# A memory gain carried as a 769th column, a rope table loaded last, and row blocks turned between two halves of a product

## The chip, the core and the metric

The kernel runs on one core of one Trainium2 chip. The core has a matrix engine (TensorE, PE in the rows; its weight loads are PEld), a vector engine (VectorE, DVE), a scalar engine (ScalarE, ACT), GpSimd (POOL), a queue engine that issues most transfers (SyncE, SP), and 16 DMA engines. The engines run their own instruction streams in order and wait for one another through semaphores. The metric is device time of one execution in microseconds (us). Before the change: 756.78 us, the median of three runs (756.1, 756.78, 756.96).

## What is computed

One decoder layer for 512 tokens of width 1024, in fp32. Cut to what the change touches:

```
h = rms_norm(x, g_mix)
q, k, v, qi, ki, wi, conv_in, qc, gate_pre = split(h @ w_in)
qi = partial_rope(qi);  ki = partial_rope(ki)          # index heads, first 8 of 32 columns turned
mem_kv = rms_norm(mem, g_mem) @ w_mem_kv                # 256 memory tokens
... sparse attention, short convolution, memory attention, gates, w_o, gated MLP, final norm
```

`rms_norm` multiplies a row by 1/sqrt(mean of squares) and by a gain per column. In the memory product the gain can sit on the contraction index, and the factor of the row can wait until after the product.

## The kernel before, in words

Every product is done with split operands: a number is kept as a rounded high part and a low rest (`split`, L155: a copy on ScalarE, then a subtraction on VectorE), and `mm3` (L145) adds three products per contraction chunk, high by high, high by low, low by high. Contraction runs over 8 chunks of 128.

The first 50 us are a start-up stage, in which SyncE's queue brings, in this order: the memory chunks `m_kv` (8 chunks, each 256 columns of the turned memory and 512 of its weights, 768 columns of 128 rows), row block 0 of x, the gain `g_mix` for all partitions (`gx`), row block 1, the weights `w_n` of the small projection (v, the index queries and keys and the index weights: 424 columns), row block 2, memory rows 0, row block 3, memory rows 1, and `par`. ScalarE's own queue issues two small transfers first: the memory gain `gm` (128 x 8, L231) and the rope table `ropeN` (128 x 32, L232).

The compute of that stage:

- For each memory chunk, ScalarE and VectorE scale it by `gm` (L280, L281) into `mT`, the weights are split, and TensorE adds to `ps_o` and `ps_mm` (L287).
- A row block of x is normalized by `norm_rows` (L165): ScalarE squares it and sums (L160), GpSimd makes the factor in two instructions (L161, L162), VectorE multiplies (L170) into `xn`. Then `turn_rows` (L173) lets TensorE transpose it, four 128 x 128 pieces at a time into a PSUM bank (`ps_at`), and splits each four into `hhi` and `hlo`.
- The loop at L321 runs over the four row blocks b. It multiplies block b by `w_n`, 8 chunks of three matmuls into `pn` (`ps_mm`, 128 x 424), and normalizes and turns block b + 2 at high priority (L329). Then it takes v and `wiN` from `pn`, copies the 288 index columns to `rn` (L335), turns the first eight of every 32 by the rope table in six small VectorE instructions (L338 to L343), and transposes `rn` on TensorE (L346, L349). For b below 2, `memory_out` (L296) squares and sums a block of memory rows and scales the memory product's results (`kr`, `vm`).

The tile `st`, which holds a row sum and its factor, has two buffers, and so has `xn`. A scheduler puts the instructions of each engine into one fixed order from its own estimate of times; `tc.high_priority` moves work up in it, and `tc.keep_in_program_order` pins an instruction to the written order. At run time each engine follows its list, whatever comes late.

After this stage come the rest of the projection (w_in), the attentions, the gates, w_o, and the MLP.

Of the kernel before, what the change touches and what calls it, by code (L numbers as in the profile page):

```python
# [10 lines left out]
F32 = mybir.dt.float32  # L11
F32R = mybir.dt.float32r
AF = mybir.ActivationFunctionType
ALU = mybir.AluOpType
# [3 lines left out]
P = 128  # L18
# [13 lines left out]
M = 256  # L32
# [41 lines left out]
class Late:  # L74
# [5 lines left out]
    def add(self, fn, extra=0):  # L80
        self.queue.append((self.now + self.lag + extra, fn))
# [9 lines left out]


@with_exitstack
def layer(ctx, tc, x, mem, g_mix, g_mem, g_ffn, g_final, w_in, w_n, m_kv, w_cm, w_att, w_o, w_up, w_down,
          params, rope, rope_n, out):
    nc = tc.nc

# [8 lines left out]
    def bank(tag="mm"):  # L106
        return ps.tile([P, 512], F32, tag=tag, name="ps_" + tag, bufs=banks[tag])
# [34 lines left out]
    def wrows(w, r, sp=wp):  # L142
        return wsplit(w[r * P:(r + 1) * P, :].rearrange("p (k c) -> p k c", c=P), sp)

    def mm3(o, sh, sl, mh, ml, first, last):  # L145
        nc.tensor.matmul(o, sh, mh, start=first, stop=False)  # L146
        nc.tensor.matmul(o, sh, ml, start=False, stop=False)  # L147
        nc.tensor.matmul(o, sl, mh, start=False, stop=last)  # L148

# [5 lines left out]
    def split(hi, lo, src):  # L155
        nc.scalar.activation(hi, src, AF.Copy)  # L156
        nc.vector.tensor_sub(lo, src, hi.bitcast(F32))  # L157
# [7 lines left out]
    def norm_rows(src, g, tmp):  # L165

        xn = tmp.tile([P, D], F32, tag="xn", name="xn", bufs=2)
        st = tmp.tile([P, 2], F32, tag="st", name="st", bufs=2)
        r = inv_rms(src, st, xn)
        nc.vector.scalar_tensor_tensor(xn, src, r, g, op0=ALU.mult, op1=ALU.mult)  # L170
        return xn

    def turn_rows(xn, dst, b, tag="at"):  # L173

        for h in range(2):
            pt = bank(tag)
            for k in range(4):
                nc.tensor.transpose(pt[:, k * P:(k + 1) * P], xn[:, (4 * h + k) * P:(4 * h + k + 1) * P], ident)
            pv = pt.rearrange("p (k s) -> p k s", s=P)
            split(dst[0][:, 4 * h:4 * h + 4, b * P:(b + 1) * P], dst[1][:, 4 * h:4 * h + 4, b * P:(b + 1) * P], pv)  # L180

    def norm_T(src, g, dst, b, tmp):
        turn_rows(norm_rows(src, g, tmp), dst, b)
# [41 lines left out]

    es = ExitStack()
    ea = es.enter_context(pool("ea", side="right"))
    gm = ea.tile([P, KD], F32, name="gm")
    gx = ea.tile([P, D], F32, name="gx")
    ropeN = ea.tile([P, 2, NB, 4], F32, name="ropeN")  # L230
    nc.scalar.dma_start(gm, g_mem)  # L231
    nc.scalar.dma_start(ropeN, rope_n)  # L232

    warm = const.tile([P, 1], F32, name="warm")
    tc.keep_in_program_order(nc.scalar.activation(warm, mhalf, AF.Copy))
# [2 lines left out]
    def first(dma):  # L238
        tc.keep_in_program_order(dma)

    def first_rows(src, b, p, tag):
        t = p.tile([P, D], F32, tag=tag, name="rows")
        first(nc.sync.dma_start(t, src[b * P:(b + 1) * P, :]))
        return t
# [5 lines left out]
    for c in range(KD // 2):  # L250

        n = 1 if c == 0 else 2
        raw = op.tile([P, 2, M + 2 * CW], F32, tag=kv_tags[c], name="mkv")
        for i in range(0, 2, n):
            first(nc.sync.dma_start(raw[:, i:i + n], m_kv[2 * c + i:2 * c + i + n].rearrange("k p c -> p k c")))
        hi = wp.tile([P, 2, 2 * CW], F32R, tag="whi", name="whi", bufs=3)
        lo = wp.tile([P, 2, 2 * CW], F32R, tag="wlo", name="wlo", bufs=3)
        mkv.append((raw, hi, lo, n))
        if c == 2:
            xin = [first_rows(x, 0, ea, "in0")]  # L260
            first(nc.sync.dma_start(gx, bcast(g_mix, D)))
# [8 lines left out]
    memn = [first_rows(mem, 0, op, "omeh")]  # L270
    xin.append(first_rows(x, 3, ea, "in3"))
    memn.append(first_rows(mem, 1, op, "omel"))


    pkv = [bank("o"), bank()]
    for c, (raw, hi, lo, n) in enumerate(mkv):
        for i in range(0, 2, n):
            for k in range(2 * c + i, 2 * c + i + n):
                src = raw[:, k % 2, :M]
                nc.scalar.activation(mh[:, k], src, AF.Copy, scale=gm[:, k:k + 1])  # L280
                nc.vector.scalar_tensor_tensor(ml[:, k], src, gm[:, k:k + 1], mh[:, k].bitcast(F32), op0=ALU.mult,  # L281
                                               op1=ALU.subtract)
            split(hi[:, i:i + n], lo[:, i:i + n], raw[:, i:i + n, M:])
            for k in range(2 * c + i, 2 * c + i + n):
                for b in range(MB):
                    bs = slice(b * P, (b + 1) * P)
                    mm3(pkv[b], mh[:, k, bs], ml[:, k, bs], hi[:, k % 2], lo[:, k % 2], k == 0, k == KD - 1)  # L287
        if c == 2:
            norm_T(xin[0], gx, h, 0, ea)
# [31 lines left out]
    for b in range(NB):  # L321
        bs = slice(b * P, (b + 1) * P)
        pn = bank()
        for i in range(4):
            for j in range(2):
                k = 2 * i + j
                mm3(pn[:, :NW], h[0][:, k, bs], h[1][:, k, bs], wn[i][1][:, j], wn[i][2][:, j], k == 0, k == KD - 1)
        if b + 2 < NB:
            with tc.high_priority(offset=800):  # L329
                norm_T(xin[b + 2], gx, h, b + 2, ea)  # L330
        split(V[:, b, :, 0:HD], V[:, b, :, HD:], pn[:, :KV].rearrange("p (g d) -> p g d", g=NG))
        nc.vector.tensor_scalar_mul(wiN[:, b, :], pn[:, NW - NIH:NW], (NIH * IDXD) ** -0.5)
        rn = ea.tile([P, NIH + 1, IDXD], F32, tag="rn", name="rn", bufs=2)
        rt = ea.tile([P, 2, NIH + 1, 4], F32, tag="rt", name="rt", bufs=2)
        nc.scalar.activation(rn, pn[:, KV:NW - NIH].rearrange("p (n d) -> p n d", d=IDXD), AF.Copy)  # L335
        cos, sin = (ropeN[:, i, b:b + 1, :].to_broadcast([P, NIH + 1, 4]) for i in range(2))
        a1, a2 = rn[:, :, 0:4], rn[:, :, 4:8]
        nc.vector.tensor_mul(rt[:, 0], a2, sin)  # L338
        nc.vector.tensor_mul(rt[:, 1], a1, sin)
        nc.vector.tensor_mul(a1, a1, cos)  # L340
        nc.vector.tensor_mul(a2, a2, cos)
        nc.vector.tensor_sub(a1, a1, rt[:, 0])
        nc.vector.tensor_add(a2, a2, rt[:, 1])  # L343
        rows_ = rn.rearrange("p n d -> p (n d)")
        pt = bank("at")
        nc.tensor.transpose(pt[:IDXD, 2 * P:3 * P], rows_[:, 2 * P:], ident)  # L346
        if b:
            for t in range(2):
                nc.tensor.transpose(pt[:, t * P:(t + 1) * P], rows_[:, t * P:(t + 1) * P], ident)  # L349
        nc.scalar.activation(rK[:, bs], pt[:IDXD, 2 * P:3 * P], AF.Copy)  # L350
        if b:
            nc.scalar.activation(rQ[:, :, (b - 1) * P:b * P], pt[:, :2 * P].rearrange("p (t s) -> p t s", t=2), AF.Copy)
        if b < MB:
            memory_out(b, kr[:, b])
        if b:
            ahead(C_CG if b == 1 else C_U if b == 2 else C_BG)
# [512 lines left out]
```

## Time and profile before

| | |
|---|---|
| median of three runs | 756.78 us |
| the profiled execution | 757.61 us |
| its span on the core | 755.8 us |
| PE busy | 740.9 us (98%), 3458 matmuls and transposes |
| DVE, ACT, POOL busy | 464.5, 340.2, 21.1 us |
| HBM read | 75.77 MB |

The profile is one execution of the program. The span is what the core's trace covers; the execution's time is 1.8 us more. A busy TensorE is not a TensorE at its peak: matmuls overlap, and their ends are modelled, so the distance from one start to the next says what one costs. An idle engine costs time only if the chain that ends last runs through the wait.

### The profile page before, as it was taken

Reading aid. Unit: us, or ns where it says so; the run is one execution under the profiler, and the core shown is the slowest. Engines: PE = TensorE matmul, PEld = TensorE weight load, DVE = VectorE, ACT = ScalarE, POOL = GpSimd, SP = SyncE. Lnnn points to the kernel's source line nnn. Section 1 sums busy time; section 2 is a strip of 40 time slices with the busy share of each in tenths; the row PEclk is TensorE's granted clock in tenths of the full one; section 3 lists DMA queues with packets and bytes.
Section 4 is the critical chain, followed back from the end, with each engine's and each line's share of the span. In section 5 each row is a group of like instructions: output and inputs, shape, how many; then the busy total and the mean of one; then the engine's idle time right before and its main releaser. Section 6 shows DMA issues by size and latency. Waiting matters only on the chain.

```text
span 755.8 us, 9168 instructions
## 1 busy us (share of the span) xinstructions
PE 740.9 (98%) x3458; PEld 618.9 (82%) x3458; DVE 464.5 (61%) x795; ACT 340.2 (45%) x568; POOL 21.1 (3%) x49
## 2 busy tenths in 40 slices
PE   6999999999999999999999999999999999999996
PEld 4888888888888888888899888888888888888884
DVE  4845999999777763386466565656565654121225
ACT  5848565676455553244235434343434443121214
POOL 0200002000000000000010000000000000000001
PEclk9999999999999999999999999999999999999998
DMA  9625234522122224344403232232323232323202
GB/s 340 221 84 172 85 111 123 170 72 76 57 91 74 74 65 161 117 139 138 142 29 99 97 97 100 91 104 88 107 86 110 83 112 76 119 84 109 86 29 112
DMA packets 25709, 81.81 MB, mean 108 GB/s; under 512 B 3424, under 2 KB 4576, under 8 KB 25664
## 3 DMA queue, kind: packets, MB, share of 16 engines
q1 hardware_dynamic: 25232, 80.94, 32.7%
q8 instruction: 27, 0.44, 0.3%
q10 hardware_dynamic: 432, 0.28, 0.1%
q14 instruction: 18, 0.15, 0.1%
HBM read 75.77 MB, written 2.10 MB: 103 GB/s over the span
## 4 chain that ended last, share of the span: by engine, by line
PE 94%; ACT 2%; DMA 1%; DVE 1%; POOL 1%; issue 1%; POOLq 0%; SPq 0%
PE ps_mm L146 19%; PE ps_mm L148 19%; PE ps_mm L147 19%; PE ps_at L146 9%; PE ps_at L148 9%; PE ps_at L147 9%; PE ps_at L625 1%; PE ps_o L656 1%; DMA mkv<-m_kv 1%; PE ps_o L147 1%; PE ps_o L148 1%; PE ps_o L146 1%; PE ps_at L642 1%; PE ps_at L420 1%; PE ps_at L556 1%
## 5 line engine op out<-in xcount | busy, mean ns | idle before, releaser
L157 DVE TENSOR_TENSOR wlo<-raw,whi 128x1024 fp32r<-128x1024 f32 (+2 forms) x122 | 144.7, 1188 | 197.1 <-ACT whi L156 197.1
L156 ACT ACTIVATE whi<-raw 128x1024 fp32r<-128x1024 f32 (+2 forms) x122 | 125.8, 1032 | 177.1 <-PE ps_o L148 82.1
L146 PE MATMUL ps_mm<-hhi,whi 128*128 128x512 f32 x312 | 122.8, 394 | 0.0
L147 PE MATMUL ps_mm<-hlo,whi 128*128 128x512 f32 x312 | 122.2, 392 | 0.0
L148 PE MATMUL ps_mm<-hhi,wlo 128*128 128x512 f32 x312 | 122.2, 392 | 0.0
L147 PE MATMUL ps_at<-h2l,whi 128*128 128x512 f32 (+1 forms) x216 | 78.9, 366 | 0.0
L148 PE MATMUL ps_at<-h2h,wlo 128*128 128x512 f32 (+1 forms) x216 | 78.8, 365 | 0.0
L146 PE MATMUL ps_at<-h2h,whi 128*128 128x512 f32 (+1 forms) x216 | 78.7, 366 | 0.0
L148 PEld LDWEIGHTS ps_mm<-hhi,wlo 128*128 128x128 f32 x312 | 58.6, 188 | 11.7
L147 PEld LDWEIGHTS ps_mm<-hlo,whi 128*128 128x128 f32 x312 | 58.6, 188 | 11.6
L146 PEld LDWEIGHTS ps_mm<-hhi,whi 128*128 128x128 f32 x312 | 58.6, 188 | 11.5
L146 PE MATMUL ps_mm<-h2h,whi 128*128 128x512 f32 x160 | 62.2, 389 | 0.0
L147 PE MATMUL ps_mm<-h2l,whi 128*128 128x512 f32 x160 | 62.2, 389 | 0.0
L148 PE MATMUL ps_mm<-h2h,wlo 128*128 128x512 f32 x160 | 62.2, 389 | 0.0
L147 PEld LDWEIGHTS ps_at<-h2l,whi 128*128 128x128 f32 x216 | 40.7, 189 | 6.6
L148 PEld LDWEIGHTS ps_at<-h2h,wlo 128*128 128x128 f32 x216 | 40.7, 189 | 6.5
L146 PEld LDWEIGHTS ps_at<-h2h,whi 128*128 128x128 f32 x216 | 40.6, 189 | 6.5
L147 PEld LDWEIGHTS ps_mm<-h2l,whi 128*128 128x128 f32 x160 | 30.0, 188 | 6.3
L148 PEld LDWEIGHTS ps_mm<-h2h,wlo 128*128 128x128 f32 x160 | 30.0, 188 | 6.2
L146 PEld LDWEIGHTS ps_mm<-h2h,whi 128*128 128x128 f32 x160 | 30.0, 188 | 6.2
L789 ACT ACTIVATE t<-t 128x512 f32<-128x512 f32 x22 | 13.9, 633 | 44.9 <-DVE t L471 44.8
L156 ACT ACTIVATE acth<-t 128x512 fp32r<-128x512 f32 x14 | 8.8, 632 | 40.4 <-DVE t L790 40.4
(266 smaller groups left out, 1316.8 us busy)
## 6 DMA issues: line engine op xcount, KB each, us to landing
raw<-w_up SPq DMA_DIRECT2D x44, 512.0 KB, 3.4
raw<-w_in SPq DMA_DIRECT2D x39, 512.0 KB, 3.4
raw<-w_down SPq DMA_DIRECT2D x22, 512.0 KB, 3.4
raw<-w_o SPq DMA_DIRECT2D x8, 512.0 KB, 3.5
raw<-w_cm SPq DMA_DIRECT2D x8, 320.0 KB, 3.0
mkv<-m_kv SPq DMA_DIRECT2D x3, 768.0 KB, 8.8
rows<-x SPq DMA_DIRECT2D x4, 512.0 KB, 10.1
x<-x SPq DMA_DIRECT2D x4, 512.0 KB, 6.4
```

The source lines that it names most:

```text
L146: nc.tensor.matmul(o, sh, mh, start=first, stop=False)
L147: nc.tensor.matmul(o, sh, ml, start=False, stop=False)
L148: nc.tensor.matmul(o, sl, mh, start=False, stop=last)
L156: nc.scalar.activation(hi, src, AF.Copy)
L157: nc.vector.tensor_sub(lo, src, hi.bitcast(F32))
L420: nc.tensor.matmul(pb[:, :W], Q4[:, hd, (b - 1) * P:b * P], K4[:, :W], start=True, stop=True)
L556: nc.tensor.matmul(pb[:, j * M:(j + 1) * M], QC[:, 2 * t + j, b * P:(b + 1) * P], KM[i][:, 2 * t + j, :], start=(i == 0), stop=(i == 1))
L625: nc.tensor.matmul(pb[:, :N], QS[:, hd, b * P:(b + 1) * P], KS[i][:, g, :N], start=(i == 0), stop=(i == 1))
L642: nc.tensor.transpose(pt[:, kb * P:(kb + 1) * P], lt[:, kb * P:(kb + 1) * P], ident)
L656: nc.tensor.matmul(po[:, q0:], V[:, kb, g, :], PT[i][:, c], start=(kb == 0 and i == 0), stop=(kb == NB - 1 and i == 1))
L789: nc.scalar.activation(tt[0], tt[0], AF.Silu)
```

## The change

The memory gain becomes column 768 of each memory chunk, so a chunk has 769 columns, and the transfer of `gm` is gone. `ropeN` is loaded by SyncE's queue after memory rows 1. In the loop over row blocks, block b + 1 (for b = 1 and 2) is normalized at the top of step b at high priority, and its transposes are written between chunks 0 to 3 and chunks 4 to 7 of the product of block b; the first transpose of each four and the first matmul of chunk 4 are pinned to the written order.

```diff
-    gm = ea.tile([P, KD], F32, name="gm")
...
-    nc.scalar.dma_start(gm, g_mem)
-    nc.scalar.dma_start(ropeN, rope_n)
...
-        raw = op.tile([P, 2, M + 2 * CW], F32, tag=kv_tags[c], name="mkv")
+        raw = op.tile([P, 2, M + 2 * CW + 1], F32, tag=kv_tags[c], name="mkv")
...
     memn.append(first_rows(mem, 1, op, "omel"))
+    first(nc.sync.dma_start(ropeN, rope_n))
...
-                src = raw[:, k % 2, :M]
-                nc.scalar.activation(mh[:, k], src, AF.Copy, scale=gm[:, k:k + 1])
...
+                src, gm = raw[:, k % 2, :M], raw[:, k % 2, M + 2 * CW:]
+                nc.scalar.activation(mh[:, k], src, AF.Copy, scale=gm)
...
         pn = bank()
+        nxt = xin[b + 1] if 0 < b < NB - 1 else None
+        if nxt is not None:
+            with tc.high_priority(offset=800):
+                nxt = norm_rows(nxt, gx, ea)
         for i in range(4):
+            if nxt is not None and i == 2:
+
+                turn_rows(nxt, h, b + 1, "at", pin=True)
             for j in range(2):
                 k = 2 * i + j
-                mm3(pn[:, :NW], h[0][:, k, bs], h[1][:, k, bs], wn[i][1][:, j], wn[i][2][:, j], k == 0, k == KD - 1)
-        if b + 2 < NB:
-            with tc.high_priority(offset=800):
-                norm_T(xin[b + 2], gx, h, b + 2, ea)
+                mm3(pn[:, :NW], h[0][:, k, bs], h[1][:, k, bs], wn[i][1][:, j], wn[i][2][:, j], k == 0, k == KD - 1,
+                    pin=nxt is not None and k == 4)
```

Lines after the change are a few higher: the transposes of `turn_rows` go from L178 to L180, those of `rn` from L346 and L349 to L353 and L356, the multiplication by the gain from L170 to L172, the six rope instructions from L338 to L343 to L345 to L350. Numbers behind names (`xn_314`) tell the buffers of one tile name apart.

TensorE before, around the end of block 1's product (`ps_mm_356`); `xn_314` is row block 2, `xn_381` row block 3, `rn_337` the index columns of block 0:

```order
L146 MATMUL ps_mm_356<-wnh3_154,hhi_80 128x424
L147 MATMUL ps_mm_356<-wnl3_155,hhi_80 128x424
L148 MATMUL ps_mm_356<-wnh3_154,hlo_81 128x424
L178 MATMUL ps_at_320<-ident_64,xn_314 128x128 x4
L178 MATMUL ps_at_327<-ident_64,xn_314 128x128 x4
L346 MATMUL ps_at_346<-ident_64,rn_337 32x128
L178 MATMUL ps_at_387<-ident_64,xn_381 128x128 x4
L146 MATMUL ps_mm_432<-wnh0_142,hhi_80 128x424
L147 MATMUL ps_mm_432<-wnl0_143,hhi_80 128x424
L178 MATMUL ps_at_394<-ident_64,xn_381 128x128 x4
```

TensorE after, around the middle of block 1's product (now `ps_mm_334`); `xn_335` is row block 2, `rn_315` the index columns of block 0:

```order
L146 MATMUL ps_mm_334<-wnh1_143,hhi_80 128x424
L149 MATMUL ps_mm_334<-wnl1_144,hhi_80 128x424
L150 MATMUL ps_mm_334<-wnh1_143,hlo_81 128x424
L353 MATMUL ps_at_324<-ident_64,rn_315 32x128
L180 MATMUL ps_at_353<-ident_64,xn_335 128x128 x4
L180 MATMUL ps_at_360<-ident_64,xn_335 128x128 x4
L146 MATMUL ps_mm_334<-wnh2_147,hhi_80 128x424
L149 MATMUL ps_mm_334<-wnl2_148,hhi_80 128x424
```

The transposes of row block 2 now stand 12 matmuls earlier, in the middle of block 1's product, and the transpose of block 0's index columns stands ahead of them there. Those of row block 3 likewise go to the middle of block 2's product, behind the transposes of block 1's index columns.

VectorE before, where row block 3 is multiplied by the gain (L170 on `xn_381`) and the index columns of block 0 are turned (`rn_337`, `rt_338`):

```order
L365 TENSOR_SCALAR par_76<-par_76 128x24
L170 SCALAR_TENSOR_TENSOR xn_381<-rows_160,st_382,gx_111 128x1024
L338 TENSOR_TENSOR rt_338<-rn_337,ropeN_112 128x36
L339 TENSOR_TENSOR rt_338<-rn_337,ropeN_112 128x36
L341 TENSOR_TENSOR rn_337<-rn_337,ropeN_112 128x9x4
L340 TENSOR_TENSOR rn_337<-rn_337,ropeN_112 128x9x4
L343 TENSOR_TENSOR rn_337<-rn_337,rt_338 128x9x4
L342 TENSOR_TENSOR rn_337<-rn_337,rt_338 128x9x4
```

VectorE after, at the same place (row block 3 is `xn_411`, the index columns of block 0 `rn_315`):

```order
L372 TENSOR_SCALAR par_76<-par_76 128x24
L345 TENSOR_TENSOR rt_316<-rn_315,ropeN_111 128x36
L346 TENSOR_TENSOR rt_316<-rn_315,ropeN_111 128x36
L348 TENSOR_TENSOR rn_315<-rn_315,ropeN_111 128x9x4
L347 TENSOR_TENSOR rn_315<-rn_315,ropeN_111 128x9x4
L172 SCALAR_TENSOR_TENSOR xn_411<-rows_157,st_412,gx_110 128x1024
L350 TENSOR_TENSOR rn_315<-rn_315,rt_316 128x9x4
L349 TENSOR_TENSOR rn_315<-rn_315,rt_316 128x9x4
```

The multiplication of row block 3 moved from ahead of the six rope instructions to between the fourth and the fifth of them. On ScalarE, the squares of a memory block and of a row block change places twice: memory rows 0 ahead of row block 2, and memory rows 1 ahead of row block 3.

## Rows read from the trace of the kernel before

**Rows 1.** Stretches: TensorE, its weight loads, VectorE, ScalarE, GpSimd, granted clock, DMA share, GB/s
```profile
8.00:12.00 4.00, 3.05 (x8) 1.60 (x6) 1.96 (x3) 2.89 (x6) 0.00 (x0) 1.00 1.01 367
...
16.00:20.00 4.00, 3.61 (x20) 2.79 (x19) 2.80 (x5) 3.89 (x8) 0.22 (x2) 1.00 1.03 419
...
36.00:100.00 64.00, 64.00 (x300) 54.10 (x299) 44.45 (x98) 37.11 (x70) 0.00 (x0) 1.00 0.37 114
100.00:748.00 648.00, 648.00 (x3029) 541.55 (x3029) 393.94 (x654) 275.19 (x446) 13.38 (x27) 1.00 0.30 97
```

**Rows 2.** Timeline of TensorE, 29 to 37 us: start, length, line, what
```profile
29.91 0.35 PE L146 MATMUL ps_mm<-wnh,hhi 128*128 128x424 f32 x1
...
32.23 1.04 PE L178 MATMUL ps_at<-ident,xn 128*128 128x128 f32 x8
33.11 0.27 PE L346 MATMUL ps_at<-ident,rn 128*32 128x128 f32 x1
33.22 0.60 PE L178 MATMUL ps_at<-ident,xn 128*128 128x128 f32 x4
34.93 0.46 PE L146 MATMUL ps_mm<-wnh,hhi 128*128 128x424 f32 x1 [1.12 <-ACT hhi L156]
...
35.53 0.66 PE L178 MATMUL ps_at<-ident,xn 128*128 128x128 f32 x4
36.01 0.46 PE L146 MATMUL ps_mm<-wnh,hhi 128*128 128x424 f32 x1
...
36.51 0.40 PE L146 MATMUL ps_mm<-hhi,whi 128*128 128x512 f32 x1
```

**Rows 3.** Timeline of ScalarE, 28 to 31 us and one row at 41 us
```profile
28.18 0.28 ACT L156 ACTIVATE v<-ps_mm 128x128 fp32r<-128x128 f32 x1
28.34 1.06 ACT L160 ACTIVATE xn<-rows 128x1024 f32<-128x1024 f32 x1
29.29 0.20 ACT L160 ACTIVATION_READ_ACCUMULATOR xn<-rows 128x1 f32 x1
29.38 1.06 ACT L160 ACTIVATE rows<-rows 128x1024 f32<-128x1024 f32 x1
...
30.43 0.41 ACT L335 ACTIVATE rn<-ps_mm 128x288 f32<-128x288 f32 x1
...
41.19 0.28 ACT L156 ACTIVATE v<-ps_mm 128x128 fp32r<-128x128 f32 x1 [4.36 <-PE ps_mm L148]
```

**Rows 4.** Timeline of VectorE, 30 to 33 us and one row at 42 us
```profile
30.44 1.28 DVE L170 SCALAR_TENSOR_TENSOR xn<-rows,st,gx 128x1024 f32<-128x1024 f32 x1 [1.21 <-POOL st L162]
31.64 0.19 DVE L338 TENSOR_TENSOR rt<-rn,ropeN 128x36 f32<-128x36 f32 x1
...
32.13 0.20 DVE L343 TENSOR_TENSOR rn<-rn,rt 128x36 f32<-128x36 f32 x1
32.24 0.19 DVE L342 TENSOR_TENSOR rn<-rn,rt 128x36 f32<-128x36 f32 x1
...
42.98 0.19 DVE L342 TENSOR_TENSOR rn<-rn,rt 128x36 f32<-128x36 f32 x1
```

**Rows 5.** Timeline of GpSimd, the factor of the second of two squares
```profile
26.86 0.55 POOL L162 TENSOR_TENSOR st<-st,mhalf 128x1 f32<-128x1 f32 x1
```

**Rows 6.** Memory rows 0: issue on SyncE's queue; KB and us to landing
```profile
13.92 0.33 SPq L243 DMA_DIRECT2D rows<-mem  x1
...
rows<-mem SPq DMA_DIRECT2D x1, 512.0 KB, 10.2
```

**Rows 7.** Waits of TensorE: for whom, us in total, times, longest
```profile
PE ps_o L147 <- DVE wlo L157: 0.9, 2, 0.5
PE ps_o L146 <- ACT whi L156: 0.6, 1, 0.6
```

**Rows 8.** Timeline of TensorE, second and third matmul of the program
```profile
5.42 0.63 PE L146 MATMUL ps_mm<-whi,mT 128*128 128x512 f32 x1
5.85 0.63 PE L147 MATMUL ps_o<-wlo,mT 128*128 128x512 f32 x1
```

## What the change should do to the time, on record before it ran

> **What bounds the kernel now.** Read the stretches first. From 36 to 748 us TensorE is busy in every microsecond [rows 1], so the time is TensorE's list of work plus what it waits in the first 36 us and the tail behind the last matmul. The order of instructions is the same before and after from the end of the small projection on, and the last 8 us are not touched. So the change is worth what it does to TensorE's waits before 36 us, and whatever it adds or saves there arrives at the end in full: behind it lies no idle time that could take it up.
>
> Second, the timeline of TensorE where the change acts [rows 2]. Block 1's product runs densely: 12 matmuls of 424 columns lie between 29.91 and 32.23, 0.193 us each. Then come eight transposes in 0.88 us (0.11 each), and trouble: between 32.23 and 36.51 TensorE does 17 transposes (1.87 us) and four matmuls (0.77 us), 2.64 us of work in 4.28. **1.64 us are lost**, 1.12 of them in the wait for `hhi` of row block 2, the rest in restarts behind transposes. That is the wait which the change is aimed at.
>
> Third, the timelines of ScalarE and VectorE [rows 3, 4], for what feeds TensorE at that place: v, two squares and the copy `rn` on ScalarE, then on VectorE the multiplication of row block 3 and the six rope instructions.
>
> **The change part by part.**
>
> *The stall that goes.* Row block 2 is transposed behind chunk 3 of block 1's product, and 12 matmuls (2.32 us) follow before block 2's product asks for `hhi`. In before the first product on row block 2 got its `hhi` at 34.93, 1.82 us after that block's eight transposes gave way at 33.11 [rows 2], with ScalarE held up by other work in between; 2.32 is more. Hidden: the 1.64 us go. If the cover were short, it would cost what is missing of it, up to 0.5 us.
>
> *The stall that comes.* Ahead of those transposes TensorE's list now has the transpose of block 0's index columns (L353), and TensorE gets there at 29.91, where it began chunk 4 before [rows 2]. In before this transpose stood 12 matmuls and eight transposes later, at 33.11, and waited for nothing. It needs all six rope instructions of block 0. When are they done? In before at 32.24 + 0.19 = 32.43 [rows 4], which is already 2.5 us too late for the new place. Now they come later still:
>
> 1. ScalarE squares memory rows 0 ahead of row block 2. The second square of that pair had its factor at 26.86 + 0.55 = 27.41 [rows 5]; now this is row block 2's, so VectorE multiplies row block 2 from 27.44 to 28.72 (1.28 us, the duration in [rows 4]).
> 2. The second pair of squares now begins with memory rows 1, whose `st` takes the one of two buffers that this multiplication frees. So it begins at 28.75, where the pair of before began at 28.34 [rows 3].
> 3. A square takes 1.04 us (28.34 to 29.38), and `rn` is copied 2.09 us after the pair's start and ends 0.41 later [rows 3]: 30.84 to 31.25.
> 4. Four rope instructions: 31.29 to 31.78 (0.49, as 31.64 to 32.13 in [rows 4]).
> 5. Then VectorE's list has the multiplication of row block 3, and the last two rope instructions are behind it. Row block 3 is now the second square: it begins at 29.79, its sum is read 1.15 later (28.34 to 29.29 + 0.20 in [rows 3]), 30.94, and the multiplication starts 0.95 after that (29.49 to 30.44, rows 3 and 4, GpSimd's two instructions lie between): 31.89. It holds VectorE for 1.20 us (30.44 to 31.64): 33.09.
> 6. Two rope instructions, 0.11 + 0.19 [rows 4]: 33.39, and with a handover of about 0.05 L353 starts at 33.44.
>
> TensorE waits from 29.91 to 33.44, **3.53 us**. From both sides: without the buffer wait of step 2 it is 3.1; with the 0.95 of step 5 doubled it is 4.5. I take 3.5, the sum of rows. Queued behind L353 are the eight transposes of row block 2 and the second half of block 1's product, and everything on TensorE after that.
>
> *The second place.* The same pattern in block 2: TensorE reaches the transposes of block 1's index columns 12 matmuls (2.32 us) after block 1's product ends. In before, the way from `v` of a block to its last rope instruction took 41.19 to 42.98 + 0.19, 1.98 us [rows 3, 4], plus some 0.1 ahead of `v`. Hidden with 0.2 us to spare; bounds 0 and 0.5. Row block 3 itself is multiplied long before.
>
> *Restarts.* The first matmul behind transposes costs about 0.11 us more (two matmuls in 0.50 us from 36.01 to 36.51, [rows 2], instead of 0.39). Those of before are in the 1.64. After has one for each of two groups, and saves one since the transposes of `rn` now join a group: +0.1.
>
> *The gain as a column.* The same scale and multiplication instructions, of the same shapes, read their factor from another tile: 0. Two transfers of 4 and 16 KB leave the head of ScalarE's queue. What they cost the memory chunks is not shown in a row of its own. TensorE's waits for the chunks' pieces are 0.9 and 0.6 us in all [rows 7], so the gain is between 0 and 1.5; the DMA engines are full in that stretch (share 1.01, 367 GB/s, [rows 1]), and 20 KB at that rate are 0.05 us. I take 0, the near end.
>
> The trace against the longer rows: a chunk row is now 769 x 4 = 3076 bytes. The rows of `w_n`, 848 x 4 = 3392 bytes and no multiple of 256 either, come in a stretch that moves 419 GB/s, more than the chunks' own 367 [rows 1]. [...]
>
> *The rope table and `par` later.* One more issue of 0.33 us on SyncE's queue, which waits for landings anyway. Memory rows 0 were issued at 13.92 and landed 10.2 later [rows 6]. Four more 512-KB places at 419 GB/s, 1.25 us each, would put the two small transfers at 18.9 and their landing at 29.1, an estimate; the first user needs them at 31.29. Spare 2.2 us, cost 0. Memory rows 0 themselves land at 24.12, 3.29 us ahead of the 27.41 of step 1, and that way takes 1.04 + 1.15 + about 0.95 = 3.14: spare 0.15, and what is missing would be added to step 1.
>
> **Sum:** 3.53 + 0.1 - 1.64 = +2.0 us. The profiled execution took 757.61 (its span 755.8), so a like one would take 759.6; it is 0.83 above the median of 756.78, and against the median the forecast is **758.8**.
>
> **The rivals.**
>
> *TensorE comes back at the lower clock.* [...] The waits up to 1.12 us in [rows 2] did not lower it, and none of 3.5 us is in the trace before the tail. [...] For it: the longest wait within the work so far. Against: TensorE's clock was not seen to fall in any wait. [...]
>
> *The second place waits as well.* If block 1's rope rows are late by 0.5 to 1 us, TensorE stands there again: 759.5. Against it the 0.2 us of spare.
>
> *Not slower: the front gains.* If the memory chunks land early enough that the 1.5 us of [rows 7] vanish, the whole chain, steps 1 to 6 with it, moves up by that much: +0.5, 757.3, no change that could be told. It decides from 0.5 us on. Against it the full DMA engines and the 0.05 us above. To come out faster, L353 would have to start before 31.4, while step 3 alone ends at 31.25 and six rope instructions need 0.8: I see no row for it. That the delay is taken up later is excluded by 100% from 36 to 748 us [rows 1].
>
> **How the numbers follow.** The forecast has 0.58, the second place 0.12, the lower clock 0.15, the front 0.11, faster 0.04. A measurement of this kernel can tell about 0.2% (1.5 us) from no change. The forecast's own bounds (3.1 to 4.5 for the wait, 0.4 either way at the front) run from +1.2 to +3.4, so some of it, 0.07, falls within 0.2%. Slower: 0.51 + 0.12 + 0.15 = 0.78; same 0.18; faster 0.04. The range goes from 757.4, near the front's case, to 761.2, near the lower clock's, and leaves about 0.2 outside.
>
> **What would show it.** In the profile after: TensorE idle for about 3.5 us ahead of L353, released by VectorE's L349 or L350; the multiplication of row block 3 between the fourth and fifth rope instruction, starting near 31.9; the first matmul of block 2's product without a wait for `hhi`; matmuls still 0.19 us apart behind the wait; chunks landing as before. I am wrong if L353 starts before 32, if the wait for `hhi` is still there, if matmuls behind the wait are 0.35 apart, or if TensorE's first dense stretch starts earlier by half a microsecond.

## The result, and the profile after

The changed kernel took 761.62 us, the median of four runs (760.9, 761.43, 761.81, 762.53), beside 756.87 for the kernel before: a ratio of 1.0065, 95% interval 1.0047 to 1.0082, slower by 4.75 us. The forecast was +2.0 us and a range up to 761.2. The profiled execution after is the 760.9 one, span 759.1 us.

The stretches after answer to [rows 1]; the 32 to 36 us line is new (TensorE, its weight loads, VectorE, ScalarE, GpSimd, granted clock, DMA share, GB/s):

```profile
8.00:12.00 4.00, 3.08 (x11) 1.94 (x10) 2.92 (x6) 3.81 (x7) 0.00 (x0) 1.00 1.01 365
16.00:20.00 4.00, 3.67 (x20) 2.82 (x19) 3.13 (x6) 3.89 (x8) 0.74 (x2) 1.00 1.03 417
...
32.00:36.00 4.00, 3.31 (x14) 3.25 (x15) 3.33 (x7) 1.50 (x4) 0.00 (x0) 0.57 0.24 71
36.00:100.00 64.00, 64.00 (x305) 54.58 (x304) 41.54 (x94) 37.54 (x72) 0.00 (x0) 1.00 0.34 105
100.00:748.00 648.00, 648.00 (x3027) 540.98 (x3026) 393.66 (x653) 273.68 (x443) 11.97 (x26) 1.00 0.30 96
```

TensorE is still busy all the time from 36 us on, and the transfers move as much as before. What is new is 0.57 in the clock's column between 32 and 36 us. TensorE's timeline there answers to [rows 2]:

```profile
28.84 0.36 PE L150 MATMUL ps_mm<-wnh,hlo 128*128 128x424 f32 x1
32.69 0.37 PE L353 MATMUL ps_at<-ident,rn 128*32 128x128 f32 x1 [3.48 <-DVE rn L349]
32.85 1.91 PE L180 MATMUL ps_at<-ident,xn 128*128 128x128 f32 x8
34.42 0.70 PE L146 MATMUL ps_mm<-wnh,hhi 128*128 128x424 f32 x1
34.92 0.56 PE L149 MATMUL ps_mm<-wnl,hhi 128*128 128x424 f32 x1
35.27 0.56 PE L150 MATMUL ps_mm<-wnh,hlo 128*128 128x424 f32 x1
35.62 0.51 PE L146 MATMUL ps_mm<-wnh,hhi 128*128 128x424 f32 x1
35.97 0.36 PE L149 MATMUL ps_mm<-wnl,hhi 128*128 128x424 f32 x1
```

The last matmul ahead of the place frees TensorE at 28.84 + 0.19 = 29.03, and L353 starts at 32.69: 3.66 us, for the reason that was forecast. Behind it the eight transposes take 1.57 us (32.85 to 34.42) in place of 0.88, and matmuls of 424 columns are 0.35 apart in place of 0.193. The granted clock is 0.50 from 33 to 35 us. In the trace of the kernel before it is 0.50 only behind the last matmul, from 752 us on. That trace's first matmuls are as far apart, column for column (0.43 us for 512 columns, [rows 8], where those from 324 to 348 us are 0.227 apart), with 1.00 in the clock's column there.

The chain behind the wait, on GpSimd, ScalarE and VectorE, answers to [rows 3 to 5] (start, length, line, what):

```profile
25.98 0.55 POOL L164 TENSOR_TENSOR st<-st,mhalf 128x1 f32<-128x1 f32 x1
```
```profile
27.89 1.06 ACT L162 ACTIVATE rows<-rows 128x1024 f32<-128x1024 f32 x1 [0.31 <-DVE xn L172]
...
28.94 1.04 ACT L162 ACTIVATE xn<-rows 128x1024 f32<-128x1024 f32 x1
...
29.98 0.39 ACT L342 ACTIVATE rn<-ps_mm 128x288 f32<-128x288 f32 x1
```
```profile
30.40 0.20 DVE L345 TENSOR_TENSOR rt<-rn,ropeN 128x36 f32<-128x36 f32 x1 [1.80 <-ACT rn L342]
...
30.75 0.19 DVE L347 TENSOR_TENSOR rn<-rn,ropeN 128x36 f32<-128x36 f32 x1
31.04 1.28 DVE L172 SCALAR_TENSOR_TENSOR xn<-rows,st,gx 128x1024 f32<-128x1024 f32 x1
32.24 0.19 DVE L350 TENSOR_TENSOR rn<-rn,rt 128x36 f32<-128x36 f32 x1
32.35 0.19 DVE L349 TENSOR_TENSOR rn<-rn,rt 128x36 f32<-128x36 f32 x1
```

These are steps 1 to 6, all 0.87 us earlier than forecast, since this execution's front was that much earlier: factor ready at 26.53 (forecast 27.41), squares from 27.89 (28.75), `rn` from 29.98 (30.84), four rope instructions, the multiplication of row block 3 at 31.04 (31.89), the last two behind it. Memory rows 0 landed 10.2 us after their issue, as in [rows 6]. TensorE's waits answer to [rows 7]; the wait of 1.1 us for `hhi` is gone, the new one stands in its place:

```profile
PE ps_at L353 <- DVE rn L349: 3.5, 1, 3.5
PE ps_o L149 <- DVE wlo L159: 0.9, 2, 0.5
```

**Where the time went.** In a timeline, the start of the same matmul can be compared between kernels. Four of them divide the program: the 36th of the small projection (the last ahead of the wait), the first on `oath`, the first of the MLP (`h2h`), and the last of all. The table gives the first start and the three distances, each from two rows of a timeline, for all traces of the study:

| kernel | 36th starts at | to `oath` | to `h2h` | to the last |
|---|---|---|---|---|
| before | 29.72 | 295.24 | 62.43 | 360.73 |
| before, second trace (e5) | 28.45 | 295.22 | 62.44 | 360.73 |
| after | 28.84 | 298.98 | 62.93 | 360.72 |
| after, second trace (e9) | 29.29 | 299.03 | 62.92 | 360.73 |
| e1 front only | 29.17 | 295.44 | 62.92 | 360.73 |
| e2 loop only | 28.33 | 299.99 | 62.44 | 360.73 |
| e3 wait filled | 29.04 | 297.45 | 62.92 | 360.73 |
| e4 rope first | 29.46 | 297.67 | 62.92 | 360.73 |
| e6 moved by 32 to 128 bytes | 29.42 | 295.45 | 62.92 | 360.73 |
| e7 gain column | 29.39 | 295.44 | 62.93 | 360.72 |
| e8 rope late | 29.44 | 295.26 | 62.44 | 360.73 |
| e10 index columns later | 28.95 | 294.53 | 62.44 | 360.73 |
| e11 moved by 256 to 1024 bytes | 29.45 | 295.23 | 62.44 | 360.72 |
| e12 moved by 64 to 256 bytes | 28.69 | 295.59 | 62.89 | 360.72 |
| e13 after, tiles placed | 28.57 | 298.62 | 62.44 | 360.73 |
| e14 filled, tiles placed | 28.68 | 297.28 | 62.44 | 360.73 |
| e15 front, tiles placed | 31.37 | 295.22 | 62.44 | 360.72 |
| e16 index columns two later | 28.84 | 293.54 | 62.44 | 360.73 |

Two readings. The first column goes from 28.3 to 29.7 (31.4 once) whatever the edit: it is the spread of the start-up between executions, and before's two traces of the same program are 1.27 apart in it. The other columns repeat to 0.02 us in the two traces of before and to 0.05 us in those of after, and so show what an edit does: from before to after the distance to `oath` grew by 3.74 us, and the one to `h2h`, where no instruction changed its place, by 0.50.

### The profile page after: what moved, and what is told of

Its sections match the earlier page's. It is cut to its first block, busy times and chain, and to the rows that moved or that the text cites. A ratio compares the mean times of both kernels' runs of the same rounds, so it can differ in the third digit from the quotient of the medians.

```text
span 759.1 us, 9163 instructions
## 1 busy us (share of the span) xinstructions
PE 742.2 (98%) x3458; PEld 620.1 (82%) x3458; DVE 464.9 (61%) x795; ACT 340.6 (45%) x568; POOL 20.1 (3%) x49
## 4 chain that ended last, share of the span: by engine, by line
PE 94%; ACT 1%; DVE 1%; issue 1%; DMA 1%; POOL 1%; POOLq 0%; SPq 0%
PE ps_mm L149 19%; PE ps_mm L146 19%; PE ps_mm L150 19%; PE ps_at L146 9%; PE ps_at L149 9%; PE ps_at L150 9%; PE ps_at L632 1%; PE ps_o L663 1%; PE ps_o L149 1%; PE ps_o L150 1%; PE ps_o L146 1%; PE ps_at L649 1%; DMA mkv<-m_kv 1%; PE ps_at L180 1%; PE ps_at L427 1%
```

## The experiments

Times are medians beside the kernel before on the same chip; the 95% interval is of the ratio. Chips differ: the kernel before has 756.39 beside e1 to e4 and 757.09 or 757.13 beside the others, so differences count and not times, also against expectations that were written with 756.4 in mind.

**e1 and e2: front and loop apart.** e1 has the loop of before and the new front; e2 the new loop and the old front.

```diff
 e1: loop as before; mkv tiles with M + 2 * CW + 1 columns, ropeN after memory rows 1
 e2: loop as after;  gm and ropeN on ScalarE's queue, mkv tiles with M + 2 * CW columns
```

> The kernel before with the change's front alone: the gain as a column of the memory chunks, the rope table loaded last, and the loop over the row blocks as before. Theory (the two small transfers at the head of ScalarE's queue delayed the memory chunks): TensorE's first matmuls and all behind them start 0.9 us earlier, as the matched instructions of the trace after do from 10.9 us on, and nothing takes it up later, so 756.87 - 0.9 = 756.0 us (755.5 to 756.4). Rival (the 0.9 us of the trace after are a difference between two executions): 756.9, first matmuls where they were. Rival (rows of 3076 bytes cost more than the transfers they save): 757.2 or more, chunks landing later.

> The kernel after with the front of the kernel before: the gain and the rope table at the head of ScalarE's queue, chunk rows of 3072 bytes; the loop is the changed one. Theory (front and loop add up): 761.6 + 0.9 = 762.5 us, TensorE's wait ahead of the transpose of block 0's index columns 3.5 to 3.7 us as in the trace after. Rival (the front has nothing to do with it): 761.6. Rival (the rope table loaded last makes the rope instructions late and the wait long): the wait is shorter by more than 0.5 us and the time is under 761.

e1: 758.05 against 756.39, ratio 1.0020 (1.0011 to 1.0029). e2: 760.42, ratio 1.0049 (1.0035 to 1.0063). Both theories failed. The front does not gain 0.9 us, it costs 1.66; of that, 0.70 us are in the distances to `oath` and `h2h` (295.44 and 62.92), and the loop alone does not have them in the second (62.44). The other 0.96 us lie outside these distances, so ahead of the 36th matmul or in the tail. The rival with the long rows named the time (757.2 or more); e7 and e15 below do not bear out its reason. e2's wait was 3.48 us as in after, so the late rope table has no part in it; its lower clock lasted longer:

```profile
32.00:36.00 4.00, 3.83 (x15) 3.75 (x16) 2.93 (x5) 1.46 (x3) 0.00 (x0) 0.50 0.34 116
36.00:40.00 4.00, 4.00 (x18) 3.80 (x17) 0.87 (x7) 0.69 (x2) 0.00 (x0) 0.76 0.04 17
```

In after the second of these stretches is at 1.00, and e13 has 0.60 and 1.00 in the two. The longer half-rate stretch is why e2's distance to `oath` is 1.4 us more than e13's, which has the same loop.

**e3 and e4: the clock and the wait.** e3 gives TensorE work in the wait; e4 takes VectorE's multiplication out from between the rope instructions.

```diff
 e3, ahead of the transpose of block 0's index columns, in its PSUM bank:
+        for n in range(32):
+            nc.tensor.transpose(pt[:, :P], ident, ident)
 e4, the factor of row block 3 (b == 2) made with an exponent that reads rn of block 0:
+                    nc.gpsimd.tensor_scalar(half, rn0[:, 0, 4:5], 0.0, -0.5, op0=ALU.mult, op1=ALU.add)
-        nc.gpsimd.tensor_tensor(out=st[:, 1:2], in0=st[:, 0:1], in1=mhalf, op=ALU.pow)
+        nc.gpsimd.tensor_tensor(out=st[:, 1:2], in0=st[:, 0:1], in1=half, op=ALU.pow)
```

> The kernel after, in its order, with 32 transposes of the identity (128 x 128, overwritten afterwards) on TensorE at the place where it waits, between chunk 3 of block 1's product and the transpose of block 0's index columns. 32 x 0.11 = 3.5 us of work lie in a wait of 3.66. [...] Rival (the clock costs nothing that stays): 761.6.

> The kernel after, with VectorE's order changed at one place: the factor of row block 3 is made to depend on block 0's last rope instruction (one more small GpSimd instruction), so that all six rope instructions of block 0 stand before the multiplication of row block 3 and not four of them. Theory (VectorE's 1.28 us multiplication between the fourth and the fifth rope instruction is the last part of TensorE's wait): the wait falls from 3.66 to about 2.2 us, the index transpose starts near 31.2; time 760.1 if the clock still falls behind it, 758.5 if it does not. Rival (ScalarE's order, not the multiplication, sets the wait): the wait stays above 3.2 and the time is 761.6.

e3: 759.74, ratio 1.0050 (1.0037 to 1.0062). Its timeline of TensorE, where the 32 transposes are the first row:

```profile
29.23 3.66 PE L327 MATMUL ps_at<-ident 128*128 128x128 f32 x32
32.88 0.27 PE L330 MATMUL ps_at<-ident,rn 128*32 128x128 f32 x1
32.98 1.03 PE L180 MATMUL ps_at<-ident,xn 128*128 128x128 f32 x8
33.77 0.44 PE L146 MATMUL ps_mm<-wnh,hhi 128*128 128x424 f32 x1
34.05 0.36 PE L149 MATMUL ps_mm<-wnl,hhi 128*128 128x424 f32 x1
34.25 0.35 PE L150 MATMUL ps_mm<-wnh,hlo 128*128 128x424 f32 x1
```

The index columns start no earlier than without the filling (3.84 us behind the 36th matmul, 3.85 in after), but transposes and matmuls behind them are at full rate again (0.79 us for eight, 0.20 apart), and the distance to `oath` is 297.45 where after has 298.98: the lower clock costs 1.5 us of its own, beside the wait. After has a granted clock of 0.57 from 32 to 36 us, behind the idle time; e3, with work without any use in that time, has 1.00 from 28 to 40 us.

e4: 760.15, ratio 1.0043 (1.0030 to 1.0056), and TensorE's wait:

```profile
PE ps_at L359 <- DVE rn L353: 2.1, 1, 2.1
```

The wait fell by 1.3 us, as the theory had it, so VectorE's multiplication was its last part. In the traced execution the clock fell behind the 2.15 us too (0.60 from 32 to 36 us), and the median is the theory's time for that case, 760.1. But two of the five runs took 758.70 and 758.99 us at a mean granted clock of 0.998, where the other three have 0.996: that is near the theory's 758.5 for a clock that stays. There is no trace of those two; they suggest that the same wait brings the lower clock in some executions and not in others.

**e5: before once more, for its trace.**

> The kernel before, unchanged, for a second trace of it. Theory (the profiled execution of before, 757.61 us, had a late front, and that is why the trace after shows a gain of 0.9 us there while the front alone costs 1.7 us in the medians): an execution near 756.4 us, whose first chunk of 768 KB is scaled near 7.6 us and not at 9.04, and whose matmuls from 12 us on start some 1.2 us earlier than in the first trace. Rival (the front of before is always like that): scaling near 9.0 again, and a time of 757 or more.

It took 756.3 us, and the second pair of scalings, which the chunk of 768 KB releases, is at 7.76 where the first trace has 9.04 (ScalarE; the first fence is the first trace, the second e5):

```profile
9.04 0.91 ACT L280 ACTIVATE mT<-mkv,gm 128x256 fp32r<-128x256 f32 x2 [3.20 <-DMA mkv<-m_kv]
```
```profile
7.76 0.91 ACT L280 ACTIVATE mT<-mkv,gm 128x256 fp32r<-128x256 f32 x2 [1.47 <-DMA mkv<-m_kv]
```

So the profiled execution of before had a late front, 1.3 us of it, and the 0.9 us that after's front seems to gain against it are this spread and no effect of the change.

**e6, e7, e8, e11 and e12: what the front's edits cost.** e6, e11 and e12 change the size of four tiles and nothing else.

```diff
 e6 (+ 1), e12 (+ 8), e11 (+ 32), on the kernel before:
-        raw = op.tile([P, 2, M + 2 * CW], F32, tag=kv_tags[c], name="mkv")
+        raw = op.tile([P, 2, M + 2 * CW + 1], F32, tag=kv_tags[c], name="mkv")
-            first(nc.sync.dma_start(raw[:, i:i + n], ...))
+            first(nc.sync.dma_start(raw[:, i:i + n, :M + 2 * CW], ...))
 e7: before with the gain as a column;  e8: before with ropeN after memory rows 1
```

> The kernel before with one column more in the four tiles of the memory chunks, which nothing loads or reads. No instruction and no transfer changes; each of the four tiles grows by 32 bytes a partition, and what is placed behind them moves by 32 to 128 bytes. Theory (the placement costs the 0.7 us by which the matmuls from 300 to 348 us are stretched in the traces of after and of the front alone, and not in that of the loop alone): 756.4 + 0.7 = 757.1 us (756.9 to 757.4), matmuls 0.231 us apart from 324 to 348 us. Rival (the rope table's or the gain's transfers change something that lasts till 348 us): 756.4, matmuls 0.2267 apart there.

> The kernel before with the gain as a column of the memory chunks, rows of 3076 bytes; the rope table stays at the head of ScalarE's queue, the loop as before. Theory (the 3076-byte rows slow the chunks: 315 to 350 GB/s from 4 to 8 us in the traces of the new front, 395 in the trace of the loop alone): most of what the front costs, +0.7 for the placement and +0.5 to +0.9 for the rows: 757.6 to 758.0 us. Rival (the rope table loaded late is what costs): 757.1, the placement alone. Rival (the gain's transfer held up the chunks and its removal helps): 756.4 or less.

> The kernel before with the rope table loaded last on SyncE's queue; the gain stays on ScalarE's queue, chunk rows of 3072 bytes, tiles placed as before. Theory (the long rows and the placement make up the front's cost, the rope table costs nothing): 756.4 us (756.0 to 756.7), matmuls 0.2267 apart from 300 to 348 us. Rival (the late rope table costs): 757 or more. Rival (the table's 16 KB held up the chunks): 755.8 or less.

> The kernel before with 32 columns more per chunk row in the four tiles of the memory chunks, which nothing loads or reads: each tile grows by 256 bytes a partition and what is placed behind them moves by 256 to 1024 bytes, where the first experiment on the placement moved it by 32 to 128. Theory (only the place within a short stretch of memory matters, so a move by a multiple of 256 bytes changes nothing): as before within 0.2 us in the trace, matmuls 0.2267 us apart from 324 to 348 us. Rival (any move counts, since it is the distance between tiles or the bank that matters): stretches of the trace become faster or slower by 0.2 to 1 us, as with the small move.

> The kernel before with 8 columns more per chunk row in the four tiles of the memory chunks, which nothing loads or reads: each tile grows by 64 bytes a partition and what is placed behind them moves by 64 to 256 bytes. Theory (the place within a line of 32 bytes matters, and these moves keep it as the 32-byte ones did): no statement on the sign; the stretches from 88 to 100 us and from 290 to 348 us show whether they behave as in the kernel before (matmuls 0.231 apart in the first, 0.2267 in the second) or as with the 32-byte move (0.2267 and 0.231). If the first, the loss belongs to the one move of 32 to 128 bytes; if the second, to any small move.

Against 757.13 and 757.09: e6 757.90 (1.0010, 1.0001 to 1.0018), e7 758.04 (1.0010, 1.0001 to 1.0019), e8 757.49 (1.0009, 1.0000 to 1.0018), e11 757.11 (1.0001, 0.9992 to 1.0010), e12 757.90 (1.0012, 1.0001 to 1.0022). The intervals overlap, so the medians alone do not part these kernels; the table does: e6 and e7 have 295.45 and 295.44, 62.92 and 62.93, what e1 has to 0.01 us, and e8 has 295.26 and 62.44, what before has to 0.04. A column that nothing loads or reads costs the whole 0.70 us, as e6's theory had it; of e7's theory only that part is left, and a cost of the late rope table (e8) is not seen behind the 36th matmul. Groups of TensorE's matmuls from 324 to 346 us, mean ns of one at the end; e6 first, then e11:

```profile
L147 PE MATMUL ps_mm<-oatl,whi 128*128 128x512 f32 x24 | 9.5, 395 | 0.0
```
```profile
L147 PE MATMUL ps_mm<-oatl,whi 128*128 128x512 f32 x24 | 9.3, 389 | 0.0
```

By the order in which the kernel makes its tiles, the move of e6 pushes `oatl`, `ocvh`, `ocvl`, `ome`, `g0`, `km` and `vm` back by 32 to 128 bytes a partition. With 256 to 1024 bytes (e11) the three distances are those of before to 0.01 us; with 64 to 256 (e12) the loss is there again, 0.82 us. So moves by multiples of 256 bytes are free here, as e11's theory had it, and the two smaller moves are not; whether multiples of 128 would do was not tried. The 0.70 us are a balance: from 88 to 100 us the matmuls of after, which has the same move, are closer than those of before (0.227 and 0.231 us apart), from 324 to 348 us it is the other way round (0.232 and 0.227). What in the placement costs the time was not tried.

**e9: after once more.**

> The kernel after, unchanged, beside the others on this chip. [...] Rival (the +4.75 of the first comparison were a chip's own): less than 3.5 above.

761.53 against 757.09, ratio 1.0061 (1.0047 to 1.0074), +4.4: the loss repeats. Three of its five runs took 761.3 to 761.5 at a mean granted clock of 0.996, the other two 762.3 and 763.3 at 0.992; the profiled e2, with the long half-rate stretch, has 0.993.

**e13, e14 and e15: do the terms close?** The tiles padded to 800 columns, the move of e11.

```diff
-        raw = op.tile([P, 2, M + 2 * CW + 1], F32, tag=kv_tags[c], name="mkv")
+        raw = op.tile([P, 2, M + 2 * CW + 32], F32, tag=kv_tags[c], name="mkv")
 e13: on after;  e14: on e3;  e15: on e1; the same 769 columns are loaded
```

> The kernel after with the four tiles of the memory chunks padded from 769 to 800 columns a row (the same 769 are loaded and read), so that what is placed behind them moves by 256 to 1024 bytes, the move that changed nothing in the kernel before, instead of 32 to 128. Theory (placement is 0.7 of the loss, wait and clock the rest): 0.7 us less than after, 3.5 to 4.1 us above before, matmuls 0.2267 us apart from 324 to 348 us. Rival (the placement's 0.7 belongs to the kernel before alone): as after, 4.4 or more above before.

> The padded tiles of 800 columns and the 32 transposes of the identity in TensorE's wait together: the kernel after without the lower clock and without the placement. Theory (what is then left is the forecast's own sum, wait of 3.5 to 3.7, restarts 0.1, stall of 1.64 gone): 2.0 us above before (1.5 to 2.5), that is 758.8 to 759.1 us. Rival (a further cost is still in the changed kernel): 3 or more above before. Rival (clock and placement overlap, so that both away gives less than their sum): 2.5 to 3.

> The front of the change alone (gain column, rope table last) with the tiles padded to 800 columns a row. Theory (the front itself costs and gains nothing that stays, the 0.7 to 1.7 us of the front alone were the placement and the spread of the first landings): within 0.5 us of before, matmuls 0.2267 us apart from 324 to 348 us. Rival (the 3076-byte rows, or the rope table on SyncE's queue, delay the chunks): 0.6 us or more above before, the third chunk scaled later than 14.5 us in the trace.

Against 757.13: e13 760.57 (1.0042, 1.0030 to 1.0055), e14 759.16 (1.0025, 1.0016 to 1.0035), e15 756.88 (0.9999, 0.9990 to 1.0008). The distance to `h2h` is back at 62.44 in all three. e14 and e15 came as their theories said, and e13, at +3.44, is 0.06 short of its theory's lower bound. With placement and clock taken out, the changed kernel is 2.03 us slower than before: the forecast's own sum. The front, once placed, is worth nothing that can be told. (e15's traced execution has a very late front and took 759.2 us, as one other of the eleven did, so its trace looks like the rival's, and the median decides; the kernel before has such times too, 759.16 beside e7 and 759.25 beside e9.) In that trace TensorE waited 1.25 us and then 0.53 us for the weights of a chunk, and its clock fell there as well. The trace of e4 has nearly the same two waits at the same place, 1.39 and 0.52 us, and its clock stayed. e15 first, then e4:

```profile
11.00 0.50 PE L146 MATMUL ps_o<-whi,mT 128*128 128x512 f32 x1 [1.25 <-ACT whi L156]
12.26 0.66 PE L147 MATMUL ps_o<-wlo,mT 128*128 128x512 f32 x1 [0.53 <-DVE wlo L157]
```
```profile
12.00:16.00 4.00, 3.74 (x9) 2.94 (x10) 3.27 (x5) 2.41 (x5) 0.74 (x2) 0.57 1.02 409
```
```profile
10.63 0.50 PE L146 MATMUL ps_o<-whi,mT 128*128 128x512 f32 x1 [1.39 <-ACT whi L158]
11.89 0.50 PE L149 MATMUL ps_o<-wlo,mT 128*128 128x512 f32 x1 [0.52 <-DVE wlo L159]
```
```profile
12.00:16.00 4.00, 4.00 (x18) 3.25 (x19) 3.09 (x4) 2.02 (x5) 0.74 (x2) 1.00 1.02 405
```

**e10 and e16: a version that gains.** The changed loop on before's front, with the index columns of a block transposed behind the next block's product (e10), and those of block 0 one product later still, with a third `rn` buffer (e16).

```diff
 e16, in the loop, behind the eight chunks of block b's product:
+        while turned and b > 1:
+            turn_index(*turned.pop(0))     # the transposes of rn and their copies to rK and rQ
...
-        pt = bank("at")
-        nc.tensor.transpose(pt[:IDXD, 2 * P:3 * P], rows_[:, 2 * P:], ident)
+        turned.append((b, rows_))
```

> The changed loop on the front of the kernel before (gain and rope table at the head of ScalarE's queue, tiles placed as before), with one place moved: the index columns of a block are transposed behind the next block's product and not ahead of the next row block's transposes. So TensorE's list has block 1's first half, the eight transposes of row block 2, block 1's second half, block 2's first half, the index columns of block 0, the transposes of row block 3, and so on. [...] Rival (something else is late next behind the transposes, the copies of hhi): a new wait of 0.5 us or more, and not more than 1 us is won. Rival (the turned block itself costs): not faster than before.

> The front of the kernel before and the changed loop, the index columns of block 0 transposed behind block 2's product, together with those of block 1, and a third buffer for rn; in the run before this one they stood ahead of row block 3's transposes and TensorE waited 0.85 us for them. Theory (the index columns are the only thing that TensorE waits for in the turned loop): no wait above 0.3 us between 20 and 45 us but those that the kernel before has too, 1.4 to 1.9 us below before, 755.2 to 755.7 where before is at 757.1. Rival (VectorE's list is late as a whole, and the next instruction waits in place of this one): 0.9 below before, as the run before this one.

e10: 756.21 against 757.09, ratio 0.9988 (0.9979 to 0.9997). Its first rival was right on the time, 0.9 us won and a new wait of 0.85 us, and not on the reason: nothing waits for `hhi`, TensorE waits once more for the rope instructions of block 0. Between the fourth and the fifth of them VectorE's list now has a split of weights (`wlo`) and two small instructions on block 1's product:

```profile
35.67 0.28 PE L328 MATMUL ps_at<-ident,rn 128*32 128x128 f32 x1 [0.85 <-DVE rn L367]
```
```profile
33.81 0.19 DVE L365 TENSOR_TENSOR rn<-rn,ropeN 128x36 f32<-128x36 f32 x1
33.92 1.22 DVE L321 TENSOR_TENSOR wlo<-raw,whi 128x1024 fp32r<-128x1024 f32 x1
...
35.43 0.19 DVE L367 TENSOR_TENSOR rn<-rn,rt 128x36 f32<-128x36 f32 x1
```

e16: 755.36 against 757.13, ratio 0.9978 (0.9969 to 0.9987), 1.8 us faster than before and some 6 faster than after. TensorE in e16:

```profile
28.84 0.35 PE L150 MATMUL ps_mm<-wnh,hlo 128*128 128x424 f32 x1
29.03 1.03 PE L180 MATMUL ps_at<-ident,xn 128*128 128x128 f32 x8
29.82 0.44 PE L146 MATMUL ps_mm<-wnh,hhi 128*128 128x424 f32 x1
...
34.54 1.03 PE L180 MATMUL ps_at<-ident,xn 128*128 128x128 f32 x8
35.33 0.44 PE L146 MATMUL ps_mm<-wnh,hhi 128*128 128x424 f32 x1
...
38.11 0.27 PE L328 MATMUL ps_at<-ident,rn 128*32 128x128 f32 x1
```

No row has a wait; the turned block does what it was meant to, and its distance to `oath` is 1.70 and 1.68 us under those of before's two traces, the forecast's 1.64.

## Why the prediction was wrong

**What held.** *The stall that goes*: 1.64 forecast, 1.68 to 1.70 measured in e16, and no wait for `hhi` in after. *The stall that comes*: 3.53 forecast, 3.66 measured; steps 1 to 6 each came within 0.03 us of their place, shifted by the front, and only the handover to TensorE was 0.15 in place of 0.05. *The second place*: the index columns of block 1 were ready at 39.44 + 0.19 and TensorE came at 39.84, the forecast's 0.2 of spare. *The sum*: +2.0 forecast, +2.03 in e14.

**What failed: the clock as a rival.** The prediction gave the lower clock a chance of 0.15, on the ground that no wait in the trace had lowered it. But the longest of those was 1.12 us, and the wait it had just worked out was three times as long; that the trace shows no fall in short waits says nothing on a long one. It happened in every trace with that wait (granted clock from 32 to 36 us: after 0.57, e2 0.50, e9 0.63, e13 0.60), and the prediction's own sign of it, matmuls 0.35 apart behind the wait, came with it. It need not come in every execution: one of e13's five runs, 759.10 us at a mean granted clock of 0.998 where the other four have 0.996, looks like one without. The stated range ends at 761.2, near this case, 2.4 us above the forecast; no run shows 2.4 as its price. The runs showed 1.4 (760.57 - 759.16, e13 and e14), and in e2's trace, where the half rate lasted longer, about 2.7 (299.99 in e2 less 297.28 in e14). It belonged into the sum.

**What failed: the gain as a column at 0.** The step weighed the transfer and the instructions, "of the same shapes", and not the tile: 32 bytes more per tile move what stands behind it, and 0.70 us in sum are lost up to 348 us, far from the change. The first paragraph's premise, that the change is worth what it does to TensorE's waits before 36 us, looked at the order of instructions and took their durations as given.

**What failed without harm: the front.** After's trace starts 0.9 us earlier, which looks like the rival "the front gains", but e15 puts the front itself at -0.25 (interval -0.8 to +0.6), and the forecast's 0 lies in that. Why the front alone (e1, on another chip) had 0.96 us more than the placement explains stays open. The prediction noted that the profiled execution lay 0.83 above the median and corrected for it in the sum, yet did not ask where in the trace those 0.83 lay; they lay in the front, and the test it named, "TensorE's first dense stretch starts earlier by half a microsecond", could not tell an effect from that spread. A cost of the 3076-byte rows is shown by no run. By the table the 36th matmul starts at 29.03 us on average in the nine traces with rows of 3072 bytes and at 29.06 in eight with 3076, the late e15 left out; with a spread of 1.3 us in that column, a few tenths of a us are not excluded either.

The terms of after, from the runs: 2.03 (wait, restarts, the stall that goes) + 1.4 (clock) + 0.70 (placement) = 4.1 in most executions, and some 1.3 more in those with the long half-rate stretch; measured 4.75 and 4.4 in two comparisons. The rest, 0.3 to 0.6, is within what the front spreads: the three distances of the table, which leave the front out, are 4.23 us longer in sum in after than in before, and 4.28 in e9.

## What to carry to other kernels

Where work is moved ahead on an in-order engine, look at what is drawn along in front of it: here the turned row block gained its 1.7 us, and a small transpose that came along, needing a late VectorE result, cost 3.7 and the clock. A wait on TensorE longer than any that the trace shows at full clock (here 1.12 us in before) is to be priced with a lower clock behind it (here 0.50 to 0.63 from 32 to 36 us, behind waits of 2.15 to 3.49 us), even if not every execution pays it. And a tile that grows by a column is an edit to every tile behind it: pad it so that the others keep their place (here to a multiple of 256 bytes), and compare stretches far from the change before calling it free.

## What the runs showed of the hardware

- Waits of 0.85 us (e10) and 1.12 us [rows 2] left TensorE's granted clock at 1.00 from 32 to 36 us; with waits of 2.15 (e4) and 3.48 us (after) that stretch has 0.60 and 0.57 in the traces. The length of a wait does not decide alone: with 1.25 and 0.53 us close to each other e15 has 0.57 from 12 to 16 us, and with 1.39 and 0.52 us at the same place e4 has 1.00. Nor is the price fixed: the five runs of e9, one program, have mean granted clocks of 0.996 (three runs, 761.3 to 761.5 us) and 0.992 (762.3 and 763.3).
- The same matmuls took 395 ns in their groups with tiles moved by 32 to 128 bytes (e6) and 389 with none moved (before), both at a granted clock of 1.00, and 389 with them moved by 256 to 1024 (e11); e6's move costs 0.70 us in sum over the program. A trace repeats this to 0.02 us, where medians of eleven runs had intervals 1.3 us wide.
- The landing of the first chunks spreads the whole kernel by 1.3 us from one execution to the next (28.45 and 29.72 for the same matmul of the same program), and with TensorE's work dense behind it, that spread arrives at the end in full (756.3 and 757.61 us for these two executions).
